# Gate products of a hybrid encoder block: nine instead of eight of sixteen row pairs by seven products, three of them with sums made by transfers

## Chip, cores, metric

The kernel runs on one core of one Trainium2 chip. The metric is the device time of one execution in microseconds (us); the kernel before has a median of 2029.64 us in three runs (2028.74 to 2030.21). The engines are named as the profile names them: PE (TensorE, matmuls), DVE (VectorE), ACT (ScalarE), POOL (GpSimd), SP (SyncE, which issues nearly all transfers).

## What is computed

One layer of a streaming encoder over 256 rows of 4096 columns:

```
xn = RMSNorm(x)
q, k, v, z_a, a_c, g_c, z_c = split(xn @ w_in)          # seven blocks of 2048 columns
y_a = RMSNorm(chunked_attention(q, k, v)) * silu(z_a)
y_c = RMSNorm(conv_module(a_c, g_c, ...)) * silu(z_c)    # ends with "@ w_pw + b_pw"
h = x + concat(y_a, y_c) @ w_out
h = h + sigmoid(RMSNorm(h) @ w_ple_gate + b) * (p @ w_ple)
out = RMSNorm(h)
```

The change concerns the two **gates** z_a and z_c: 256 x 4096 times 4096 x 2048 each.

## The kernel before

**Products.** All operands are split into a high part (rounded to fp32r) and a low part (the rest), and a product is three matmuls: high x high, low x high, high x low. The left operand is kept in SBUF, transposed, as tiles `big_t` of four blocks of 128 columns, in both parts. A weight block of 128 rows by two column blocks of 512 is loaded from HBM into `wt`, split by ACT (`wh`, L204) and DVE (`wl`, L205), and used at once. `wt` has 5 buffers, `wh` and `wl` have 3.

**Seven products.** `mixed_product` computes 256 rows by two column blocks of 512. It walks over 16 pairs of weight blocks (w0, w1). For a *plain* pair it makes 8 products (24 matmuls of 128x512, L385). For a pair marked `*` it makes seven products by a scheme of Strassen's kind (21 matmuls), P1 to P7, in the order P1, P5, P7, P2, P3, P6, P4. The three matmuls of one product take the high part, the low part of the left operand, and the low part of the weight or sum. For this DVE forms sums of weight blocks in two tiles: `ua` (w0's column blocks added, L467, and one of w0 and one of w1 added, L468) and `ub` (L474, L475). Both are split like weights (`uh` and `ul`, two buffers each). P5 and P7 read `ua`, P6 and P4 read `ub`, P1 reads w0, P2 and P3 read w1. The left side needs combinations of the blocks of x, made once per pair by `combine_again` (L291, then four operations of 128 columns at L268 to L271, then a split at L276 and L277).

**Transferred sums.** A pair marked `+` is also made by seven products, but its `ua` comes from two transfers: SP loads one summand (L420), then POOL issues an accumulating transfer that adds the other (L421). `sums_ahead` asks for them up to two pairs ahead, right behind the loads of the pair at hand. Of w0 only one column block is loaded then. Products ahead of the gates use such pairs; the gates do not.

**Order of the work.** An order is written out as a string; the gates use `dense`, `1 0* 3 2* 5 4* 6* 7 8* 9 10* 11 12* 14* 13 15`: eight pairs by seven products. A scheduler turns the program into one queue for each engine; within a queue the order is fixed. The stages around the change are: the products for attention and convolution, the product with `w_pw` (two calls of `mixed_product`, its left operand in `uS`, four big tiles of the pool `more`), then the combinations of x for pairs 4 to 14, then `gated` four times (two column pairs of z_a, two of z_c), and the product with `w_out`. The gates' sums `ua` and `ub` both come from the pool `lpool` with two buffers. At the end of a gate product DVE takes the four accumulators (L1067) and ACT applies silu (L1068). The multiplication with y (L184) is put into a list `later` and issued during the next product. At the start of the first gate product its four accumulators must first be emptied of the last `w_pw` product (L1043).

In the last gate product `y_ahead` makes the first operand of `w_out`, `yT[0]`, at the last pair of the order. It takes the fourth buffer of `more`.

Of the kernel before, what the change touches and what calls it, by code (L numbers as in the profile page):

```python
# [10 lines left out]
F32 = mybir.dt.float32  # L11
F32R = mybir.dt.float32r
# [4 lines left out]
P = 128  # L17
NB = 512
# [7 lines left out]
def hybrid_block(  # L26
# [310 lines left out]
    norm = units("1 3 5 7 9 11 0+ 13 2* 15 4+ 8 6* 10 12 14")  # L337
    norm_fills = (7, 8, 8, 8, 6, 4, 2, 3, 2, 3, 2, 2, 0, 6, 5, 5)
    final = units("1 0* 3 2* 5 4* 6* 7 8* 9 10* 12* 11 13 14 15")
    late = units("1 3 5 7 9 11 13 15 0* 2 4* 6 8* 10* 12 14")  # L340

    def mixed_product(
        w, col, lhs, comb, order, on_helpers, ahead=None, fills=(0,), on_begin=None, apart=NB,
        left=(), begin=None, after_sevens=lambda: None,
    ):


# [58 lines left out]
        def sums_ahead(n):  # L406
            for m in range(n, min(n + 3, len(order))):
                if order[m][1] != "+" or m in sums:
                    continue
                ua = sums[m] = upool.tile([P, 2, NB], F32, tag="u", name="ua")  # L410
                rows = w[2 * order[m][0] * P : (2 * order[m][0] + 1) * P, :]
                step = P * rows.ap[0][0]

                def columns(first, step):
                    return bass.AP(
                        tensor=rows.tensor, offset=rows.offset + first,
                        ap=[list(rows.ap[0]), [step, 2], [1, NB]],
                    )

                nc.sync.dma_start(ua, columns(col + apart, 0))  # L420
                nc.gpsimd.dma_start(ua, columns(col, step + apart), accum_op=ALU.add)  # L421
# [7 lines left out]
        for n, (pair, seven) in enumerate(order):  # L429
            if n < done:  # L430
                continue
            if ahead:
                ahead(pair)
            wts = []
            for k in range(2):
                wt = wpool.tile([P, 2, NB], F32, tag="w", name="wt")
                if seven == "+" and k == 0:
                    nc.sync.dma_start(wt[:, 0], w[2 * pair * P : (2 * pair + 1) * P, col : col + NB])
                else:
                    nc.sync.dma_start(wt, two_columns(w, 2 * pair + k, col, apart))  # L440
                wts.append(wt)
            sums_ahead(n)
            if n >= len(order) - n_left:
                for k in range(2):
                    tiles = left[2 * (n - len(order) + n_left) + k]
                    held.append((2 * pair + k, parts_of(wts[k], 2, tiles and tiles())[0]))
                fill(fills[n % len(fills)])
                continue
            if not seven:
                for k in range(2):  # L450
                    add_plain(n, k, *parts_of(wts[k], 2)[0])
                fill(fills[n % len(fills)])
                continue
            begins = not helper
            if begins:
                for name in ("P1", "P5", "P7", "P6"):
                    helper[name] = ps_tmp.tile([P, NB], F32, tag="tmp", name=f"acc_{name}")
                banks.update(helper)
            w0, w1 = wts
            plus = partial(nc.vector.tensor_tensor, op=ALU.add)  # L460
            before = list(recent)
            w0h, w0l = parts_of(w0, 1)[0]
            if seven == "+":
                ua = ub = sums[n]
            else:
                ua = ub = upool.tile([P, 2, NB], F32, tag="u", name="ua")
                plus(ua[:, 0], w0[:, 0], w0[:, 1])  # L467
                plus(ua[:, 1], w0[:, 1], w1[:, 1])  # L468
            with queued_behind(before if seven == "+" else ()):
                uah, ual = pair_parts(ua)  # L470
            w1h, w1l = parts_of(w1, 2)[0]
            if seven == "*" and not sums:
                ub = upool.tile([P, 2, NB], F32, tag="u", name="ub")
            plus(ub[:, 0], ua[:, 0], w1[:, 1])  # L474
            plus(ub[:, 1], ub[:, 0], w1[:, 0])  # L475
            ubh, ubl = pair_parts(ub)
            first = len(made)

            def s_of(i):
                t, at = comb[pair] if isinstance(comb, dict) else (comb[pair // 4], pair % 4)  # L480
                return [t[:, at + i // 2, q, (i % 2) * P : (i % 2 + 1) * P] for q in range(2)]

            k0, k1 = 2 * pair, 2 * pair + 1
            add("P1", block(k0, 0), (w0h[:, 0], w0l[:, 0]), n, True)
            add("P5", s_of(1), (uah[:, 0], ual[:, 0]), n, True)
            add("P7", s_of(0), (uah[:, 1], ual[:, 1]), n, True)
            add("P2", block(k1, 0), (w1h[:, 0], w1l[:, 0]), n, True)
            add("P3", s_of(3), (w1h[:, 1], w1l[:, 1]), n, True)
            add("P6", s_of(2), (ubh[:, 0], ubl[:, 0]), n, True)
            add("P4", block(k1, 1), (ubh[:, 1], ubl[:, 1]), n, True)  # L490
            if begins and on_begin:
                on_begin()
            if begins:
                tc.add_manual_dep(
                    made[first].ins, last_transpose[0].ins.name,
                    mybir.DependencyInfo(mybir.DependencyClass.NoSync, mybir.DependencyReason.DATA),
                    reason="transposes before the helpers take their banks",
                )
            if n == last_seven:
                on_helpers(helper)  # L500
                after_sevens()
            fill(fills[n % len(fills)])
# [270 lines left out]
    def layer_norm_swish():  # L773
# [67 lines left out]
        def split(c, i):  # L841
            if i == 0:
                assert more is not None
                uS.append(big_tile(more))
            hi, lo = uS[c][:, i, 0, :], uS[c][:, i, 1, :]
            nc.scalar.copy(hi, conv[c][:, i, :])
            nc.vector.tensor_tensor(lo, conv[c][:, i, :], hi.bitcast(F32), ALU.subtract)
# [107 lines left out]
    def heads(*parts, order=None, fills=early_fills, **kw):  # L955
# [6 lines left out]
        for (o, g), t in zip(parts, tiles):  # L962
            if o == o_v:
                vs[g] = t
            else:
                (queries_of if o == o_q else keys_of)(g, t)

    def open_late():

        nonlocal more  # L970
        first_sums.close()
        more = pool("more", 4)

    n_g = H // GH
    assert n_g == CW // NB == 4
# [69 lines left out]
        y_c.extend(ys)  # L1045
    nc.scalar.activation(idle_out, ssq_c[:, 0, 1:2], AF.Silu)
    r_c = rstd_of(ssq_c, CW, "r_c")


    xS = [xS[0][0]]  # L1050
    for c in range(2, D // NB):
        if c % 2 == 0:
            comb_tile(xS, 1)
        combine_again(xS[c // 2], 2 * (c % 2), xT[c], 0, sum_rows())()

    def gated(ys, c0, col, r_y, order, ahead):

        _, z = sum_tiles()

        def on_helpers(helper):  # L1060
            nc.scalar.copy(z[0][0], helper["P1"])
            helper_sums(helper, z)

        acc = mixed_product(w_in0, col + c0 * NB, xT, xS, order, on_helpers, ahead=ahead, fills=(2,))
        for h, j in QUARTERS:
            zz, y = z[h][j], ys[c0 + j][:, h]
            tt(zz, acc[h][j], zz, ALU.subtract if j else ALU.add)  # L1067
            nc.scalar.activation(zz, zz, AF.Silu, scale=r_x[:, h : h + 1])  # L1068
            if len(y.shape) == 3:
                zz = zz.rearrange("q (g d) -> q g d", d=HD)  # L1070
            later.append(partial(stt, y, y, r_y[:, h : h + 1], zz, ALU.mult, ALU.mult))

    def before_last(make):

        return lambda pair: make(0) if pair == dense[-1][0] else None

    yT, yS = [], []

    def y_ahead(pair):
        while len(yT) < min(pair // 2 + 2, D // NB):  # L1080
            c = len(yT)
            if c == D // NB - 2:
                fill(len(later))
            y, g, at = (y_a[c], ga, 4 * c) if c < len(y_a) else (y_c[c - len(y_a)], gc, 4 * (c - len(y_a)))
            operand(
                y, g[:, at : at + 4], c, yT, yS, None if c else more, combined=c < D // NB - 1
            )
        if pair == late[9][0]:

# [3 lines left out]
            )  # L1093
            later.append(lambda: rest.pop()())

    for ys, o_z, r_y in ((y_a, o_za, r_a), (y_c, o_zc, r_c)):
        for c0 in range(0, len(ys), 2):
            last = ys is y_c and c0 + 2 == len(ys)
            gated(
                ys, c0, o_z, r_y, dense,  # L1100
                before_last(y_ahead) if last else None,
            )


# [5 lines left out]
    def embedding():  # L1110

        pin = spool.tile([P, NH, PLE], F32, tag="row", name="pin", bufs=3)
        nc.sync.dma_start(pin, p[0, 0].rearrange("(h q) n -> q h n", q=P))
        pT.append(big_tile(more))
        for b, pt in enumerate(transposed(pin, range(PLE // P))):
            split_from_psum(pT[0], b, pt, 1.0)

# [234 lines left out]
```

## Time and profile before

| what | us |
|---|---|
| median of three runs | 2029.64 |
| the profiled execution's own time | 2028.23 |
| its span (first to last instruction) | 2026.5 |
| mean clock granted to TensorE | 0.998 |
| gate products, from 986 to about 1313 in the span | four of about 82 each |

All positions given later are us from the start of the span. The profiled execution lies 1.41 us below the median of the runs. Differences are worked out in the profiled execution and then applied to the median. A matmul's listed duration (390 ns) overlaps the next one's: their distance, not their duration, is what they cost. The same holds, more weakly, for DVE: one instruction's listed duration overlaps the next by some 80 ns.

### The profile page before, as it was taken

Reading aid. Unit: us, or ns where it says so; the run is one execution under the profiler, and the core shown is the slowest. Engines: PE = TensorE matmul, PEld = TensorE weight load, DVE = VectorE, ACT = ScalarE, POOL = GpSimd, SP = SyncE. Lnnn points to the kernel's source line nnn. Section 1 sums busy time; section 2 is a strip of 40 time slices with the busy share of each in tenths; the row PEclk is TensorE's granted clock in tenths of the full one; section 3 lists DMA queues with packets and bytes.
Section 4 is the critical chain, followed back from the end, with each engine's and each line's share of the span. In section 5 each row is a group of like instructions: output and inputs, shape, how many; then the busy total and the mean of one; then the engine's idle time right before and its main releaser. Section 6 shows DMA issues by size and latency. Waiting matters only on the chain.

```text
span 2026.5 us, 26195 instructions
## 1 busy us (share of the span) xinstructions
PE 2010.8 (99%) x9073; PEld 1654.4 (82%) x9073; DVE 1903.4 (94%) x2708; ACT 1215.0 (60%) x1583; POOL 46.9 (2%) x50
## 2 busy tenths in 40 slices
PE   9999999999999999999999999999999999999997
PEld 7888888888888888788888888888888888888876
DVE  7999999889999997888899999999999999999998
ACT  7655545655655555776556556666665666655555
POOL 0000000000000000000000000000000000000000
PEclk9999999999999999999999999999999999999999
DMA  8787878678678867456666666676666656666765
GB/s 295 222 238 234 255 217 250 177 247 240 188 221 246 252 198 241 156 177 209 196 208 207 208 204 211 208 239 210 203 211 197 208 194 201 208 218 207 231 207 180
DMA packets 171168, 436.70 MB, mean 215 GB/s; under 512 B 13966, under 2 KB 17182, under 8 KB 171034
## 3 DMA queue, kind: packets, MB, share of 16 engines
q1 hardware_dynamic: 161952, 417.93, 63.9%
q0 software_dynamic: 8432, 16.25, 4.8%
q8 instruction: 71, 1.16, 0.2%
q10 hardware_dynamic: 650, 0.84, 0.1%
q14 instruction: 63, 0.52, 0.1%
HBM read 430.77 MB, written 4.19 MB: 215 GB/s over the span
## 4 chain that ended last, share of the span: by engine, by line
PE 95%; DVE 3%; issue 1%; ACT 1%; DMA 0%; POOLq 0%; POOL 0%; ACTq 0%; SPq 0%; DVEq 0%
PE acc L385 73%; PE acc_P L385 17%; PE tmp_ps L170 1%; DVE cv L724 1%; PE acc L229 1%; DVE wl L205 1%; PE tmp_ps L893 0%; PE tmp_ps L877 0%; PE tmp_ps L911 0%; PE tmp_ps L916 0%; PE acc L373 0%; ACT wh L204 0%; PE tmp_ps L892 0%; DVE ul L205 0%; DMA xin<-in_x_dram 0%
## 5 line engine op out<-in xcount | busy, mean ns | idle before, releaser
L385 PE MATMUL acc<-wh,big_t 128*128 128x512 f32 x4154 | 1283.3, 391 | 0.6 <-DVE y_c L1043 0.4
L204 ACT CAST wh<-wt 128x1024 fp32r<-128x1024 f32 (+1 forms) x737 | 710.1, 974 | 523.3 <-PE acc L385 364.3
L385 PEld LDWEIGHTS acc<-wh,big_t 128*128 128x128 f32 x4154 | 777.0, 188 | 160.8 <-DVE y_c L1043 0.9
L205 DVE TENSOR_TENSOR wl<-wt,wh 128x1024 fp32r<-128x1024 f32 (+1 forms) x737 | 817.4, 1122 | 39.9 <-ACT wh L204 33.6
L385 PE MATMUL acc<-wl,big_t 128*128 128x512 f32 x2077 | 801.9, 391 | 0.1
L385 PEld LDWEIGHTS acc<-wl,big_t 128*128 128x128 f32 x2077 | 389.5, 188 | 82.5 <-DVE wl L205 1.8
L204 ACT CAST uh<-ua 128x1024 fp32r<-128x1024 f32 x174 | 182.9, 1052 | 91.1 <-DVE ua L468 46.3
L205 DVE TENSOR_TENSOR ul<-ua,uh 128x1024 fp32r<-128x1024 f32 x174 | 212.0, 1219 | 9.6 <-ACT uh L204 8.1
L724 DVE SCALAR_TENSOR_TENSOR cv<-uT,dw,cv 128x250 f32<-128x250 f32 (+19 forms) x480 | 203.6, 464 | 1.1
L385 PE MATMUL acc_P<-uh,big_t 128*128 128x512 f32 x528 | 161.8, 392 | 0.0
L204 ACT CAST uh<-ub 128x1024 fp32r<-128x1024 f32 x92 | 96.8, 1052 | 95.5 <-DVE ub L475 79.2
L205 DVE TENSOR_TENSOR ul<-ub,uh 128x1024 fp32r<-128x1024 f32 x92 | 112.2, 1220 | 6.7 <-ACT uh L204 5.6
L385 PEld LDWEIGHTS acc_P<-uh,big_t 128*128 128x128 f32 x528 | 98.0, 188 | 23.2 <-ACT uh L204 3.7
L385 PE MATMUL acc_P<-ul,big_t 128*128 128x512 f32 x264 | 101.3, 392 | 0.0
L467 DVE TENSOR_TENSOR ua<-wt 128x512 f32<-128x512 f32 x102 | 69.9, 685 | 17.3 <-DMA wt<-in_w_in_dram 10.7
L385 PE MATMUL acc<-uh,big_t 128*128 128x512 f32 x266 | 82.5, 390 | 0.0
L385 PE MATMUL acc_P<-wh,big_t 128*128 128x512 f32 x266 | 82.1, 389 | 0.0
L468 DVE TENSOR_TENSOR ua<-wt 128x512 f32<-128x512 f32 x102 | 69.6, 683 | 4.3 <-DMA wt<-in_w_in_dram 3.6
L385 PE MATMUL acc_P<-uh,comb_t 128*128 128x512 f32 x228 | 70.1, 390 | 0.1
L475 DVE TENSOR_TENSOR ub<-ub,wt 128x512 f32<-128x512 f32 x92 | 63.0, 685 | 0.8
L474 DVE TENSOR_TENSOR ub<-ua,wt 128x512 f32<-128x512 f32 x92 | 62.9, 683 | 0.3
L385 PEld LDWEIGHTS acc_P<-ul,big_t 128*128 128x128 f32 x264 | 49.3, 188 | 12.5 <-DVE ul L205 2.0
(243 smaller groups left out, 1485.5 us busy)
## 6 DMA issues: line engine op xcount, KB each, us to landing
wt<-in_w_in_dram SPq DMA_DIRECT2D x416, 512.0 KB, 4.5
wt<-in_w_out_dram SPq DMA_DIRECT2D x128, 512.0 KB, 4.3
wt<-in_w_ple_gate_dram SPq DMA_DIRECT2D x128, 512.0 KB, 4.2
wt<-in_w_pw_dram SPq DMA_DIRECT2D x32, 512.0 KB, 4.8
ua<-in_w_in_dram SPq DMA_DIRECT2D x31, 512.0 KB, 4.3
ua<-in_w_in_dram POOLq DMA_DIRECT2D x31, 512.0 KB, 8.7
wt<-in_w_in_dram SPq DMA_DIRECT2D x31, 256.0 KB, 2.8
hc<-in_x_dram SPq DMA_DIRECT2D x8, 512.0 KB, 4.7
```

The costliest lines, as they stand in the source:

```text
L170: nc.tensor.transpose(pt[:, i * T + h * P : i * T + (h + 1) * P], src[:, h, b] if len(src.shape) == 4 else src[:, h, b * P : (b + 1) * P], ...
L204: nc.scalar.copy(wh[:, :kc, :], wt[:, :kc, :]),
L205: nc.vector.tensor_tensor(wl[:, :kc, :], wt[:, :kc, :], wh[:, :kc, :].bitcast(F32), ALU.subtract),
L229: nc.tensor.matmul(acc, a, b[:, k, :], start=kb == 0 and kind == 0, stop=kb == kblocks - 1 and kind == 2,)
L385: nc.tensor.matmul(banks[name], a, b, start=name not in begun, stop=final and ends[name] == n and kind == 2 and not (left and name in "P2 ...
L467: plus(ua[:, 0], w0[:, 0], w0[:, 1])
L468: plus(ua[:, 1], w0[:, 1], w1[:, 1])
L474: plus(ub[:, 0], ua[:, 0], w1[:, 1])
L475: plus(ub[:, 1], ub[:, 0], w1[:, 0])
L724: nc.vector.scalar_tensor_tensor(cv[:, i, PAD - k :], uT[:, i, : T + k - PAD], dw[:, b, k : k + 1], cv[:, i, PAD - k :], ALU.mult, ALU.add,)
```

## The change

The gates' order becomes `nine`: nine pairs by seven products, of which 4, 10 and 15 (`4+`, `10+`, `15+`) have transferred sums. Pair 15 becomes a pair by seven products, and for it a ninth combination of x is made once, after the others. Room for it comes from `more`, which shrinks from four to three buffers. The fourth place becomes a pool of its own that is used three times in turn: first for the fourth tile of `uS` (`more_last`), then for the ninth combination and a single buffer for the transferred sums (`gate_place`), then for `yT[0]` and later the embedding's tile (`y_place`). `ub` in the gates is always a fresh tile of `lpool`.

```diff
+    nine = units("1 0* 3 2* 4+ 6* 5 8* 7 10+ 12* 9 14* 15+ 11 13")
...
-                ua = sums[m] = upool.tile([P, 2, NB], F32, tag="u", name="ua")
+                ua = sums[m] = (sums_in or upool).tile([P, 2, NB], F32, tag="u", name="ua")
...
-            if seven == "*" and not sums:
+            if (seven == "*" and not sums) or sums_in:
                 ub = upool.tile([P, 2, NB], F32, tag="u", name="ub")
...
-                uS.append(big_tile(more))
+                uS.append(big_tile(more if c < 3 else last_more[0][1]))
...
-        more = pool("more", 4)
+        more = pool("more", 3)
+        last_more.append(last_place("more_last"))
...
+    last_more.pop()[0].close()
+    gate_place, gate_pool = last_place("gate_place")
...
+    xS = {2 * c: (xS[c // 2], 2 * (c % 2)) for c in range(D // NB)}
+    xS[15] = gate_pool.tile([P, 2, 2, T], F32R, tag="ninth", name="comb_x"), 0
+    combine_again(*xS[15], xT[7], 2, sum_rows())()
...
-        acc = mixed_product(w_in0, col + c0 * NB, xT, xS, order, on_helpers, ahead=ahead, fills=(2,))
+        acc = mixed_product(
+            w_in0, col + c0 * NB, xT, xS, order, on_helpers, ahead=ahead, fills=(2,),
+            sums_in=gate_pool,
+        )
...
+    def open_y(pair):
+
+        gate_place.close()
+        last_more.append((None, pool("y_place", 1)))
+        y_ahead(pair)
...
-                ys, c0, o_z, r_y, dense,
-                before_last(y_ahead) if last else None,
+                ys, c0, o_z, r_y, nine,
+                before_last(open_y, nine) if last else None,
```

More of the change, by code (lines that the diff above doesn't have):

```diff
@@ L343, in mixed_product @@
         w, col, lhs, comb, order, on_helpers, ahead=None, fills=(0,), on_begin=None, apart=NB,
-        left=(), begin=None, after_sevens=lambda: None,
+        left=(), begin=None, after_sevens=lambda: None, sums_in=None,
     ):
@@ L966, in heads, with last_place @@
                 (queries_of if o == o_q else keys_of)(g, t)
+    last_more = []
+    def last_place(name):
+        place = ExitStack()
+        return place, pool(name, 1, place)
     def open_late():
@@ L1071, in gated, with before_last @@
             later.append(partial(stt, y, y, r_y[:, h : h + 1], zz, ALU.mult, ALU.mult))
-    def before_last(make):
-        return lambda pair: make(0) if pair == dense[-1][0] else None
+    def before_last(make, order=dense):
+        return lambda pair: make(0) if pair == order[-1][0] else None
     yT, yS = [], []
@@ L1085, in y_ahead @@
             operand(
-                y, g[:, at : at + 4], c, yT, yS, None if c else more, combined=c < D // NB - 1
+                y, g[:, at : at + 4], c, yT, yS, None if c else last_more[0][1], combined=c < D // NB - 1
             )
@@ L1113, in embedding @@
         nc.sync.dma_start(pin, p[0, 0].rearrange("(h q) n -> q h n", q=P))
-        pT.append(big_tile(more))
+        pT.append(big_tile(last_more[0][1]))
         for b, pt in enumerate(transposed(pin, range(PLE // P))):
```

## The prediction

> **What bounds the kernel now.** I read the page's head first, then the busy times of the four gate products, then who waited in them.
>
> ```profile
> PE 2010.8 (99%) x9073; PEld 1654.4 (82%) x9073; DVE 1903.4 (94%) x2708; ACT 1215.0 (60%) x1583; POOL 46.9 (2%) x50
> ...
> PE 95%; DVE 3%; issue 1%; ACT 1%; DMA 0%; POOLq 0%; POOL 0%; ACTq 0%; SPq 0%; DVEq 0%
> ```
>
> PE is busy 99% and carries 95% of the chain that ended last; DVE is busy 94%. A busy PE row alone proves little, because its durations overlap. So the next view cuts the gate stage into stretches of 81.60 us; its columns are length, PE, PEld, DVE, ACT, POOL busy, granted clock, DMA share, GB/s. The last row is an earlier stage with transferred sums, for comparison.
>
> ```profile
> 987.30:1068.90 81.60, 81.60 (x360) 67.57 (x361) 75.92 (x91) 50.02 (x58) 0.69 (x1) 1.00 0.64 204
> 1068.90:1150.50 81.60, 81.60 (x362) 67.57 (x361) 78.59 (x94) 49.37 (x55) 0.00 (x0) 1.00 0.65 208
> ...
> 629.00:680.00 51.00, 50.98 (x228) 41.98 (x228) 51.00 (x84) 25.21 (x27) 2.74 (x3) 1.00 0.83 246
> ```
>
> A gate product has 8 x 21 + 8 x 24 = 360 matmuls, and 81.60/360 = **0.2267 us** is one matmul at full clock. DVE is busy 78.59 of 81.60: 3.0 us a product are free. Who waited, first for PE (980 to 1319), then for DVE (1068 to 1319):
>
> ```profile
> PE acc L385 <- DVE y_c L1043: 0.4, 1, 0.4
> ```
> ```profile
> DVE ua L467 <- DMA wt<-in_w_in_dram: 4.7, 5, 1.5
> DVE wl L205 <- ACT wh L204: 2.8, 6, 0.7
> ```
>
> PE waits once, 0.4 us at the start of the gates, and then never: the stage is PE's. DVE is the close second.
>
> **The change part by part.**
>
> *Matmuls.* Each gate product has nine sevens: 9 x 21 + 7 x 24 = 357. Four products save 12 matmuls: 12 x 0.2267 = **-2.72 us**, all on the path. This is most of what can be gained.
>
> *DVE's work.* What an instruction occupies is the distance to the next in a full queue:
>
> ```profile
> 1084.05 1.22 DVE L205 TENSOR_TENSOR ul<-ub,uh 128x1024 fp32r<-128x1024 f32 x1
> ...
> 1085.79 2.35 DVE L205 TENSOR_TENSOR wl<-wt,wh 128x1024 fp32r<-128x1024 f32 x2
> 1088.06 0.69 DVE L468 TENSOR_TENSOR ua<-wt 128x512 f32<-128x512 f32 x1
> 1088.66 0.69 DVE L205 TENSOR_TENSOR wl<-wt,wh 128x512 fp32r<-128x512 f32 x1
> ```
>
> Two wide splits (1024) take 2.27, so **1.135** each; a sum or narrow split (512) takes **0.605**. A plain pair costs DVE two wide splits, 2.27, and PE 24 x 0.2267 = 5.44. A `*` pair costs three wide and five narrow, 6.43, and PE 4.76. A `+` pair saves two narrow, 5.22. Before: 8 x 6.43 + 8 x 2.27 = 69.6 a product; after: 6 x 6.43 + 3 x 5.22 + 7 x 2.27 = 70.1. DVE gains 0.5 while PE's product shrinks to 357 x 0.2267 = 80.9, so 3.0 us free become 1.8: on average it still fits. ACT (50 of 82) is not close.
>
> *The third seven in a row.* The average is not what counts; DVE's lead over PE is. A plain pair adds 3.17 to it, a `*` takes 1.67, a `+` 0.46. `dense` never has more than two sevens in a row; `nine` has `2* 4+ 6*`. After its sixth pair the lead gained since the start is 0.87 us; after 6* in `dense`, one plain pair later, it is 2.83. Here is how little was left at that place in the second product (DVE's split of 6*'s second sum, and PE's first matmul that reads it):
>
> ```profile
> 1100.98 1.22 DVE L205 TENSOR_TENSOR ul<-ub,uh 128x1024 fp32r<-128x1024 f32 x1
> ```
> ```profile
> 1102.80 0.39 PE L385 MATMUL acc_P<-ul,big_t 128*128 128x512 f32 x1
> ```
>
> It ended at 1102.20 and was read at 1102.80: 0.6 us to spare. For the new order I count from 2*, which both orders reach in the same way: its second sum's split started at 1084.05 (quoted), its low part was read at:
>
> ```profile
> 1087.84 0.39 PE L385 MATMUL acc_P<-ul,comb_t 128*128 128x512 f32 x1
> ```
>
> In the changed program's DVE queue, from behind that split to the end of 6*'s second split, stand eight narrow and eight wide instructions: 8 x 0.605 + 8 x 1.135 = 13.92. Among the wide ones are both splits of plain pair 5, which the scheduler put ahead of 6*'s last. So that split ends at 1084.05 + 1.135 + 13.92 + 0.09 (its tail) = 1099.20. PE reads 42 matmuls after 1087.84; but the scheduler also moved six other matmuls ahead of this one (five in the first product): 48 x 0.2267 = 10.88, at 1098.72. DVE is **0.5 us late**, once in each of products 2 to 4: +1.5. Bounds: 0 (a few tenths in either sum) and 1.8 a product (0.5 plus the 1.36 of the six matmuls, if what was moved ahead is late too).
>
> *The start of the gates, first product.* PE lost time as it entered the stage, waiting for DVE to empty an accumulator:
>
> ```profile
> 985.78 0.39 PE L385 MATMUL acc<-wl,big_t 128*128 128x512 f32 x1
> 986.00 0.61 PE L385 MATMUL acc<-wh,big_t 128*128 128x512 f32 x2
> 986.46 0.39 PE L385 MATMUL acc<-wl,big_t 128*128 128x512 f32 x1
> 987.28 0.73 PE L385 MATMUL acc<-wh,big_t 128*128 128x512 f32 x2 [0.43 <-DVE y_c L1043]
> 987.85 0.39 PE L385 MATMUL acc<-wl,big_t 128*128 128x512 f32 x1
> ```
>
> The row of 985.78 is w_pw's last matmul, 986.00 the gates' first. From 986.46 three distances took 1.39 instead of 0.68: 0.71 lost. The new queue issues the four L1043 in a row, with a wide split behind them that stood between them before:
>
> ```profile
> 981.33 0.69 DVE L468 TENSOR_TENSOR ua<-wt 128x512 f32<-128x512 f32 x1 [0.98 <-DMA wt<-in_w_in_dram]
> ...
> 984.81 0.68 DVE L1043 TENSOR_TENSOR y_c<-acc,row 128x512 f32<-128x512 f32 x1
> 985.41 1.21 DVE L205 TENSOR_TENSOR wl<-wt,wh 128x1024 fp32r<-128x1024 f32 x1
> 986.55 1.88 DVE L1043 TENSOR_TENSOR y_c<-acc,row 128x512 f32<-128x512 f32 x3
> ...
> 989.59 0.16 DVE L551 TENSOR_REDUCE r_c<-ssq_c 128x2 f32<-128x8 f32 x1
> 989.78 0.17 DVE L138 TENSOR_SCALAR r_c<-r_c 128x2 f32<-128x2 f32 x1
> ```
> ```profile
> 967.65 0.28 DVE L268 TENSOR_TENSOR comb<-comb 128x128 f32<-128x128 f32 x1
> 967.85 0.28 DVE L269 SCALAR_TENSOR_TENSOR comb<-comb 128x128 f32<-128x128 f32 x1
> ```
>
> The ninth combination puts about 1.4 us ahead of them (one narrow, four of 128 columns at 0.2, the distance in the last two rows), of which the idle 0.98 at 981 takes most; they start at about 985.3, and each accumulator is free before PE comes. I take **-0.71** (bounds -0.71 and 0). From 985.3 the new queue needs 14 narrow, eight wide and r_c's two (0.4), 17.95, to the end of 2*'s second split, and seven narrow and eight wide, 13.32, from there to the end of 6*'s: 1016.6. PE, without its wait, reads there at 986.0 + 2 x 5.44 + 3 x 4.76 + 22 x 0.2267 = 1016.15: 0.45 late. On top comes the first transferred sum:
>
> ```profile
> ua<-in_w_in_dram SPq DMA_DIRECT2D x31, 512.0 KB, 4.3
> ua<-in_w_in_dram POOLq DMA_DIRECT2D x31, 512.0 KB, 8.7
> ```
> ```profile
> 983.78 0.33 SPq L440 DMA_DIRECT2D wt<-in_w_in_dram  x1
> ...
> 986.65 0.33 SPq L440 DMA_DIRECT2D wt<-in_w_in_dram  x1
> ```
>
> Its place is that of `uS`'s fourth tile, so SP, behind the load of 983.78, waits for the last w_pw matmul, 985.78 + 0.39 = 986.2. With 4.3 and 8.7, and some tenths for two issues, it has landed at about 999.5 to 1000.5; DVE wants it at 985.3 + 14.5 (12 narrow, six wide and r_c's 0.4) = 999.8. I add 0.5: **+1.0** in the first product (bounds 0 and 2.2). The next weight load, which SP issued at 986.65, moves by some 0.2, and five `wt` buffers cover that; POOL's r_c waits behind the accumulate, and nobody reads r_c before the third product.
>
> *Transfers.* Direct ones cost 63.9% of the span for 417.93 MB, accumulating ones 4.8% for 16.25 MB:
>
> ```profile
> q1 hardware_dynamic: 161952, 417.93, 63.9%
> q0 software_dynamic: 8432, 16.25, 4.8%
> ```
>
> That is 3.1 and 6.0 us of all engines per MB. A `+` adds 0.26 MB net of direct and 0.52 MB of accumulating transfer, 3.9 us; three a product lift the share from 0.65 to 0.80. In the row from 629 to 680 above it was 0.83 with PE at 50.98 of 51.00. The later sums are asked for some 14 us and more before DVE's use, one buffer being free as soon as the sum before is split; I cost them at nothing. [...]
>
> *The rest.* The three-buffer pool gives the later tiles places that are long free; `yT[0]` waits for 15+, which PE passes a plain pair earlier. Both 0.
>
> **Sum.** -2.72 - 0.71 + 1.0 + 1.5 = **-0.9**: 2028.23 becomes 2027.3, and the median 2029.64 becomes **2028.7**.
>
> **Rivals.**
>
> *B, DVE is never late.* PE has no new wait: -3.43, 2026.2. For it: no PE wait in the gates now, and 0.5 is the difference of two sums of 11 and 14 us. Against it: only 0.6 was to spare with two sevens in a row.
>
> *C, DVE becomes the bound at 6*; slower.* Loads land later in busier queues (4.0 us in the gates, 4.6 from 300 to 930, where sums were transferred):
>
> ```profile
> wt<-in_w_in_dram SPq DMA_DIRECT2D x121, 512.0 KB, 4.0
> ```
> ```profile
> wt<-in_w_in_dram SPq DMA_DIRECT2D x186, 512.0 KB, 4.6
> ```
>
> DVE's sums L467 stand early in its queue and block it while they wait for a load; from 987 to 1300, in us and times:
>
> ```profile
>   DMA wt<-in_w_in_dram: 8.0, 10
> ```
>
> Ten waits each 0.6 longer are 1.5 a product. If all falls ahead of 6*, it is -3.43 + 2.5 + 3 x 2.0 = +5.1, 2034.7. It decides from 0.86 us of PE wait a product. Against it: in my count the loads of 4+, 6* and 5 land some 4 us ahead of use.
>
> *D, the first sum lands late.* The slowest accumulate took 9.9 instead of 8.7: 1.2 more in the first product, 2029.9.
>
> ```profile
> DMA to landing us min/median/max: 6.5/8.7/9.9
> ```
>
> That the change doesn't happen is no rival: the built queues hold the 12 matmuls less.
>
> **How the numbers follow.** Forecast 0.50, B 0.20, C 0.20, D 0.07, something not foreseen 0.03. A measurement of this kernel tells about 0.2%, 4.06 us, from no change: 2025.6 to 2033.7 is "same". Forecast, B, D and a fifth of C (a wait between 0.86 and 1.8 a product) lie inside: 0.81. Slower: 0.17, C's other four fifths and 0.01 of the unforeseen. Faster: the other 0.02, since all that can go here is 3.43 us. The range, 2025.9 to 2033.0, runs from B less 0.3 of the runs' own spread to the lower part of C, leaving out about 2 in 10.
>
> **What would show it.** Gate products of 357 matmuls in 80.9 us plus a wait; PE waits put down to DVE `ul` or `ub` at 6*, four times, about 0.5 each and 1.0 in the first; no wait for L1043; DMA share near 0.80. I am wrong if PE waits at another pair, if it waits for nothing, or if DVE's idle in the gates grows.

## The result, and the profile after

The changed kernel takes **2036.77 us** (median of seven runs, 2033.85 to 2038.18); the kernel before, on the same chip, 2029.91 us (2028.74 to 2032.04). The ratio is 1.0032 with a 95% interval of 1.0022 to 1.0042: slower by 6.9 us, where 1 us less was forecast, and above the range. The profiled execution is the fastest of the seven (2033.85 us, span 2032.1), so the trace shows the mild form: 5.6 us more of span than before. What the other runs lost beyond that, 2.9 us in the median, no trace here shows.

The page's busy line and its chain:

```profile
PE 2011.4 (99%) x9061; PEld 1652.8 (81%) x9061; DVE 1908.6 (94%) x2714; ACT 1223.1 (60%) x1592; POOL 62.3 (3%) x62
...
PE 92%; DVE 4%; issue 2%; DMA 1%; ACT 1%; POOLq 0%; POOL 0%; ACTq 0%; DVEq 0%
```

The 12 matmuls are gone (9061 for 9073). PE's share of the chain fell from 95% to 92%, and DMA has a share at all. The page doesn't say where; what PE waited for between 930 and 1340 does (total us, times, longest):

```profile
PE acc L386 <- DVE z L1084: 3.7, 3, 2.7
PE acc_P L386 <- DVE ul L205: 1.4, 3, 0.7
PE acc_P L386 <- ACT uh L204: 0.7, 1, 0.7
```

L1084 is the drain: four DVE instructions at a product's end that take the sums out of the accumulators (L1067 before). PE waits for it three times, at the start of products 2, 3 and 4; before, never. The rows of PE there and at the third seven in a row:

```profile
1007.75 0.50 PE L386 MATMUL acc_P<-ul,big_t 128*128 128x512 f32 x1 [0.70 <-DVE ul L205]
...
1015.83 0.74 PE L386 MATMUL acc_P<-uh,big_t 128*128 128x512 f32 x2 [0.72 <-ACT uh L204]
...
1068.26 0.39 PE L386 MATMUL acc<-wl,big_t 128*128 128x512 f32 x1
1069.11 0.70 PE L386 MATMUL acc<-wh,big_t 128*128 128x512 f32 x2 [0.47 <-DVE z L1084]
1069.65 0.40 PE L386 MATMUL acc<-wl,big_t 128*128 128x512 f32 x1
...
1096.25 0.50 PE L386 MATMUL acc_P<-ul,big_t 128*128 128x512 f32 x1 [0.33 <-DVE ul L205]
...
1150.71 0.39 PE L386 MATMUL acc<-wl,big_t 128*128 128x512 f32 x1
1151.67 0.70 PE L386 MATMUL acc<-wh,big_t 128*128 128x512 f32 x2 [0.57 <-DVE z L1084]
1152.21 0.39 PE L386 MATMUL acc<-wl,big_t 128*128 128x512 f32 x1
...
1178.81 0.50 PE L386 MATMUL acc_P<-ul,big_t 128*128 128x512 f32 x1 [0.33 <-DVE ul L205]
...
1233.27 0.39 PE L386 MATMUL acc<-wl,big_t 128*128 128x512 f32 x1
1236.37 0.84 PE L386 MATMUL acc<-wh,big_t 128*128 128x512 f32 x2 [2.71 <-DVE z L1084]
1237.00 0.63 PE L386 MATMUL acc<-wl,big_t 128*128 128x512 f32 x1
1237.43 1.05 PE L386 MATMUL acc<-wh,big_t 128*128 128x512 f32 x2
1238.28 0.63 PE L386 MATMUL acc<-wl,big_t 128*128 128x512 f32 x1
...
1239.99 0.72 PE L386 MATMUL acc<-wh,big_t 128*128 128x512 f32 x2
1240.55 0.40 PE L386 MATMUL acc<-wl,big_t 128*128 128x512 f32 x1
```

What a wait costs is read from distances of starts, not from the bracket at a row's end. From 1068.26 to 1069.65 run three matmuls, 0.68 us at 0.2267; it took 1.39, so 0.71 is lost, though the bracket says 0.47. In product 3 it is 0.82. In product 4, twelve matmuls (2.72) took 7.28: **4.56 lost**. Of these, 2.9 are the pause itself (3.10 from start to start), and 1.7 come because for some 4 us after the pause a matmul took 0.43 us instead of 0.2267. Together the three starts cost 6.1 us. That is about as much as the whole delay, since the other losses and gains nearly cancel (point 8 below).

Why the drain is late is to be read on DVE, ahead of it:

```profile
1226.48 0.69 DVE L468 TENSOR_TENSOR ua<-wt 128x512 f32<-128x512 f32 x1 [1.19 <-DMA wt<-in_w_in_dram]
...
1231.33 0.69 DVE L469 TENSOR_TENSOR ua<-wt 128x512 f32<-128x512 f32 x1 [2.42 <-DMA wt<-in_w_in_dram]
1231.94 0.68 DVE L475 TENSOR_TENSOR ub<-ua,wt 128x512 f32<-128x512 f32 x1
1232.66 0.69 DVE L476 TENSOR_TENSOR ub<-ub,wt 128x512 f32<-128x512 f32 x1
1233.27 1.22 DVE L205 TENSOR_TENSOR wl<-wt,wh 128x1024 fp32r<-128x1024 f32 x1
1234.40 1.22 DVE L205 TENSOR_TENSOR ul<-ua,uh 128x1024 fp32r<-128x1024 f32 x1
1235.54 2.48 DVE L1084 TENSOR_TENSOR z<-acc,z 128x512 f32<-128x512 f32 x4
```

L468 and L469 are the sums of the **next** product's first pair, 0*. The scheduler put them ahead of this product's drain. They stand 1.19 and 2.42 us for the two loads of 0*, with the drain queued behind. In the kernel before the same order stood there, and the loads came nearly in time (L467 and L468 are the same two sums, L1067 the drain):

```profile
1223.52 0.69 DVE L467 TENSOR_TENSOR ua<-wt 128x512 f32<-128x512 f32 x1 [0.19 <-DMA wt<-in_w_in_dram]
...
1225.90 0.69 DVE L468 TENSOR_TENSOR ua<-wt 128x512 f32<-128x512 f32 x1
...
1230.11 2.47 DVE L1067 TENSOR_TENSOR z<-acc,z 128x512 f32<-128x512 f32 x4
```

The queues of SP and POOL show what came between (the row of 1218.82 holds three loads; the last two, at 1222.08 and 1223.99, are those of 0*):

```profile
1217.50 0.38 SPq L421 DMA_DIRECT2D ua<-in_w_in_dram  x1
1218.82 5.50 SPq L441 DMA_DIRECT2D wt<-in_w_in_dram  x3
```
```profile
1223.45 1.22 POOL L422 DMA_DIRECT2D ua<-in_w_in_dram  x1 [22.22 <-DVE z L514]
```

The request at 1217.50 is for the sum of 4+, four pairs later; the accumulating half of it leaves POOL at 1223.45, between the two loads that DVE needs first. The five weight loads that SP issued between 1216 and 1230 landed after (min/median/max us), in the changed kernel and then in the one before:

```profile
DMA to landing us min/median/max: 4.4/5.3/7.3
```
```profile
DMA to landing us min/median/max: 3.4/3.8/4.3
```

The 7.3 is the second load of 0*: issued at 1223.99, landed at 1231.3, which is when L469 starts.

### The profile page after: what moved, and what is told of

Its sections match the earlier page's. It is cut to its first block, busy times and chain, and to the rows that moved or that the text cites. A ratio compares the mean times of both kernels' runs of the same rounds, so it can differ in the third digit from the quotient of the medians.

```text
span 2032.1 us, 26246 instructions
## 1 busy us (share of the span) xinstructions
PE 2011.4 (99%) x9061; PEld 1652.8 (81%) x9061; DVE 1908.6 (94%) x2714; ACT 1223.1 (60%) x1592; POOL 62.3 (3%) x62
## 4 chain that ended last, share of the span: by engine, by line
PE 92%; DVE 4%; issue 2%; DMA 1%; ACT 1%; POOLq 0%; POOL 0%; ACTq 0%; DVEq 0%
PE acc L386 70%; PE acc_P L386 17%; DVE wl L205 1%; DVE cv L725 1%; PE tmp_ps L170 1%; DMA wt<-in_w_in_dram 1%; PE acc L229 1%; DVE ul L205 1%; PE tmp_ps L894 0%; PE tmp_ps L878 0%; PE tmp_ps L912 0%; PE tmp_ps L917 0%; PE acc L374 0%; ACT wh L204 0%; PE tmp_ps L893 0%
## 5 line engine op out<-in xcount | busy, mean ns | idle before, releaser
L386 PE MATMUL acc<-wh,big_t 128*128 128x512 f32 x4098 | 1267.9, 392 | 3.9 <-DVE z L1084 3.7
L386 PEld LDWEIGHTS acc<-wh,big_t 128*128 128x128 f32 x4098 | 767.1, 188 | 162.8 <-ACT wh L204 4.1
L386 PE MATMUL acc<-wl,big_t 128*128 128x512 f32 x2049 | 791.6, 392 | 0.1
L386 PEld LDWEIGHTS acc<-wl,big_t 128*128 128x128 f32 x2049 | 384.6, 188 | 81.2 <-DVE wl L205 1.4
L204 ACT CAST uh<-ua 128x1024 fp32r<-128x1024 f32 x178 | 187.1, 1052 | 109.6 <-DVE ua L469 63.2
L205 DVE TENSOR_TENSOR ul<-ua,uh 128x1024 fp32r<-128x1024 f32 x178 | 216.9, 1219 | 10.1 <-ACT uh L204 9.3
L204 ACT CAST uh<-ub 128x1024 fp32r<-128x1024 f32 x96 | 101.0, 1052 | 78.3 <-DVE ub L476 66.2
L205 DVE TENSOR_TENSOR ul<-ub,uh 128x1024 fp32r<-128x1024 f32 x96 | 117.1, 1220 | 7.5 <-ACT uh L204 6.8
L422 POOL DMA_DIRECT2D ua<-in_w_in_dram x43 | 52.6, 1222 | 975.6 <-DMA ua<-in_w_in_dram 284.8
L468 DVE TENSOR_TENSOR ua<-wt 128x512 f32<-128x512 f32 x94 | 64.4, 685 | 13.0 <-DMA wt<-in_w_in_dram 8.4
L469 DVE TENSOR_TENSOR ua<-wt 128x512 f32<-128x512 f32 x94 | 64.3, 684 | 5.2 <-DMA wt<-in_w_in_dram 5.1
```

The lines of the kernel that those rows point to most:

```text
L204: nc.scalar.copy(wh[:, :kc, :], wt[:, :kc, :]),
L205: nc.vector.tensor_tensor(wl[:, :kc, :], wt[:, :kc, :], wh[:, :kc, :].bitcast(F32), ALU.subtract),
L386: nc.tensor.matmul(banks[name], a, b, start=name not in begun, stop=final and ends[name] == n and kind == 2 and not (left and name in "P2 ...
```

## The experiments

**Theory 1**: the traffic of a transferred sum, asked for too early, delays the next product's first loads; DVE's queue stands still for them ahead of the drains. **Theory 2**: nine pairs by seven products simply are more than DVE can do beside 80.9 us of PE, at 6* above all. Differences below are of medians, against runs of the kernel before on the same chip.

**Order of the pairs.** Eight pairs by seven products as before, three of them with transferred sums:

```diff
-    nine = units("1 0* 3 2* 4+ 6* 5 8* 7 10+ 12* 9 14* 15+ 11 13")
+    nine = units("1 0* 3 2* 4+ 6* 5 7 8* 9 10+ 11 12* 14+ 13 15")
```

> The gates go back to eight pairs by seven products, but three of them keep transferred sums in the same place and at the same points of the order (4+ fifth, 10+ tenth; 14+ in the place of 15+). VectorE has about 3.6 us less work in each product than in the kernel before (six narrow sums of 0.605 us). Theory 1 (the traffic of the transferred sums makes the loads of the next product's pair 0 late, and VectorE's queue waits for them ahead of the four instructions that empty the accumulators): TensorE still waits at the starts of products 2 to 4, 1 to 4 us in all, and the time is 1 to 6 us above before. Theory 2 (VectorE simply has too much work in the gates, at 6* above all): no wait, time within 0.5 us of before.

2042.9 us, ratio 1.0067 (1.0052 to 1.0082): worse than either theory allows. With 14+ only three pairs behind 10+ and one buffer for the sums, other things broke as well (SP stood 44.6 us for DVE's splits ahead of narrow loads, 8.1 in the changed kernel), so this is no clean test. It does show that sums by transfer can cost 13 us where DVE has *less* to do than in the kernel before, which speaks against theory 2. DVE stood 41 us for weight loads there, but whether traffic or SP's late issue made them late isn't shown.

```diff
+    nine = units("1 0* 3 2* 5 4+ 6* 7 8* 10+ 9 12* 14* 15+ 11 13")
```

> The changed kernel with an order that has no three sevens in a row near the start: 1 0* 3 2* 5 4+ 6* 7 8* 10+ 9 12* 14* 15+ 11 13. Theory 2: the waits at 6* (2.1 us in the changed kernel's profile) go away and most of the loss with them, 2030 to 2034. Theory 1: only those 2.1 us go, the waits at the product starts stay as they are, 2034 to 2036.

2033.16, ratio 1.0017 (1.0008 to 1.0027). That is 3.1 of the 6.9 us back, and inside the range of theory 2, not of theory 1. The trace says more than the time: the waits at 6* are gone, those for the drain stay (1.29, 1.50 and 0.76 us, 3.6 in all for 3.7 before the edit), and `ul`, the low part of a sum, brings new ones in products 1 and 2 (1.55 and 0.55). No half-speed matmuls follow here. So the third seven in a row is a real cost, but a kernel without it still waits for its drains and is still 3.8 us behind.

**The drain first.** The first sums of a product (L468, L469) are queued behind the last drain of the product before:

```diff
+            emptied = list(drains) if begins else []
...
+                with queued_behind(emptied):
                     plus(ua[:, 0], w0[:, 0], w0[:, 1])
                     plus(ua[:, 1], w0[:, 1], w1[:, 1])
...
+            drains[:] = [tt(zz, acc[h][j], zz, ALU.subtract if j else ALU.add)]
```

> The changed kernel, with the next product's sums for pair 0 queued on VectorE behind the last instruction that empties the accumulators, instead of ahead of it. Theory 1: the waits at the product starts (0.5, 0.6 and 2.7 us in the changed kernel's profile) and the half-speed matmuls behind the longest go away, 4 to 6 us less than the changed kernel: 2030.5 to 2032.5; the waits at 6* (0.3 to 0.7 each) stay. Theory 2: the order of these few instructions does not matter, 2036 to 2037.

2030.67, ratio 1.0007 (0.9998 to 1.0017): 5.6 us of the 6.9 are back, as theory 1 expected, and no wait for a drain is left.

**The request later.** `pin` keeps SP's request for a sum behind the weight loads that the program names before it; nothing else changes:

```diff
-                nc.sync.dma_start(ua, columns(col + apart, 0))
+                first = nc.sync.dma_start(ua, columns(col + apart, 0))
+                if sums_in:
+                    pin(first)
```

> The changed kernel with each transferred sum's first transfer kept behind the weight loads that stand ahead of it in the program: the request for the next product's 4+ moves from behind that product's first load to behind its sixth. Theory 1: pair 0's loads land in time, the waits at the product starts go away, 2030.5 to 2033. Theory 2: unchanged, 2036 to 2037. A third outcome, worse than 2037: the sum itself then lands too late for 4+.

2029.2, ratio 1.0001 (0.9992 to 1.001): 7.1 us back by a later place for the sums' requests on SP. Its queue near the same boundary, the landing of the four weight loads that SP issued there between 1216 and 1230, and PE's waits from 980 to 1340:

```profile
1223.45 7.45 SPq L443 DMA_DIRECT2D wt<-in_w_in_dram  x3
1230.95 0.43 SPq L421 DMA_DIRECT2D ua<-in_w_in_dram  x1
```
```profile
DMA to landing us min/median/max: 3.5/3.6/3.9
```
```profile
PE acc_P L386 <- ACT uh L204: 0.8, 1, 0.8
PE acc_P L386 <- DVE ul L205: 0.4, 1, 0.4
PE acc L386 <- DVE z L1086: 0.4, 1, 0.4
```

The request moved from 1217.50 to 1230.95. The bytes of the stage are the same and the DMA share of a product is 0.78 (0.77 before the edit): what changed is not how much is transferred, but when.

**What in the request costs?** First GpSimd's accumulating transfer is left out in the gates (so twelve sums lack an addend), with SP's request still early. Then it is there again, but as a plain copy over the first addend (twelve sums are one addend alone):

```diff
-                nc.gpsimd.dma_start(ua, columns(col, step + apart), accum_op=ALU.add)
+                if not sums_in:
+                    nc.gpsimd.dma_start(ua, columns(col, step + apart), accum_op=ALU.add)
```

> The changed kernel with GpSimd's accumulating transfer left out in the gates: SP still asks for the first addend of each sum at the same place of its queue, the second addend is not added, so twelve sums lack it. If it is the accumulate's traffic that makes the next product's first loads late (theory 1a), the boundary waits go and the time is 2028 to 2031. If it is the place of the request in SP's queue, its own load and SP standing still for its buffer (theory 1b), the waits stay at about 1 to 2 us each and the time is 2032 to 2036. Theory 2 (DVE's work alone): no change from the changed kernel, 2034 to 2037.

```diff
-                nc.gpsimd.dma_start(ua, columns(col, step + apart), accum_op=ALU.add)
+                if sums_in:
+                    nc.gpsimd.dma_start(ua, columns(col, step + apart))
+                else:
+                    nc.gpsimd.dma_start(ua, columns(col, step + apart), accum_op=ALU.add)
```

> The changed kernel with GpSimd's second transfer kept in place, queue and size in the gates, but as a plain copy over the first addend instead of an accumulation, so twelve sums are one addend alone. If it is the bytes that delay the next product's first loads, the boundary waits stay: 2032 to 2036. If it is the accumulating kind, which takes 6.0 instead of 3.1 us of the 16 engines per MB, they shrink to about half or go: 2028.5 to 2031.5.

Without it 2029.38, ratio 1.0003 (0.9994 to 1.0012); as a plain copy 2034.24, ratio 1.0025 (1.0016 to 1.0035). PE's waits for the drain in the first and in the second:

```profile
PE acc L386 <- DVE z L1085: 0.2, 1, 0.2
```
```profile
PE acc L386 <- DVE z L1087: 3.3, 2, 1.7
```

So it is the second 512 KB on top of the first that makes the loads late, not SP's place alone; a plain copy costs 5.1 us, an accumulation 6.9 (the slowest weight load issued between 1216 and 1230 takes 5.2, 6.0 and 7.3 us without it, with a copy, with an accumulation). The bet on the accumulating kind was wrong. That SP also stands still for the single buffer (10.8 us in seven waits) costs nothing by itself: it does so in the run without the second transfer too (11.4 us).

**No transfers at all.** All nine pairs `*`:

> Nine sevens a product with all sums on DVE: no transferred sum in the gates, three more sums and splits of 0.605 us each a `+` pair less, DVE some 3.6 us a product more than in the changed kernel, 82 against PE's 80.9. Theory 1: no late load at the boundary, PE waits for DVE's splits and drains by what DVE lacks, 1 to 2 us a product: 2030 to 2036. Theory 2 (DVE's work is what cost the time): clearly slower than the changed kernel, 2038 and more.

2032.51, ratio 1.0017 (1.0008 to 1.0026). This is against theory 2: with some 3.6 us *more* work for DVE in each product, by the expectation's count, the kernel is faster than the changed one, which loses 6.9. DVE is busy 80.1 to 81.2 of 82 us in the products, PE's listed waits are 1.3 us in all, and the kernel is 3.6 us slower than before: hardly any of DVE's time is free here. Transferred sums that come at the right time (2029.2 above, 0.2 us under its base) are worth 3.8 us against that.

**Both mends and their limits.** First the late request and the order of 2033.16 together:

> Both edits together: the sums' request stays behind the weight loads ahead of it, and 4+ and 6* are parted by a plain pair. Theory 1 (the early request makes the next product's first loads late; 6* is a second, separate and smaller cost): the boundary waits go, as with the late request alone, and so do the 0.4 to 0.8 us waits at 6*; the 1.6 and 0.6 us waits that this order brought in products 1 and 2 may stay. 2026.5 to 2029, PE waits in the gates under 2.5 us in all. Theory 2 (DVE simply has too much work in the gates, wherever it stands): the waits come back elsewhere, 2029 to 2031, no better than the late request alone at 2029.2.

2042.08, ratio 1.0063 (1.005 to 1.0077), far outside both expectations. Now the request was too late: DVE stood 3.4 to 4.6 us in products 2 to 4 for the sum of 4+ itself (14.6 us in four waits), because DVE was ready for 4+ of the last product 12 us after SP issued its request (19 us in the run of 2029.2), while the sum's two transfers took 16. Asked for one pair earlier:

```diff
-            for m in range(n, min(n + 3, len(order))):
+            for m in range(n, min(n + (4 if sums_in and not sums else 3), len(order))):
```

> The order without three sevens in a row and the late request, as in the run of 2042.1 us, but 4+ of each product asked for one pair earlier in SP's line. There DVE stood 3.4 to 4.6 us for the sum of 4+ itself, in products 2 to 4. If a transferred sum has a window (asked for too early its traffic delays the next product's first loads, too late it is itself late), those waits go and with them some 8 us: 2030 to 2035, what is left being waits for loads. If the sum was late for another reason (busy queues), it is still late: 2038 to 2043.

2030.89, ratio 1.0011 (1.0002 to 1.002): those waits are gone, 11 us with one place in a queue. Here 4+ of the last product came 19 us after its request, in the changed kernel 37. So the transferred sums had a window with two sides: 12 us ahead of DVE's use was too late, 19 was in time, and 37 made the loads beside them late. Then the late request and the drain first, in the changed kernel's own order:

> The changed kernel's own order, late request, and the next product's first sums behind the drains. Theory 1: the last 0.4 us of boundary wait go, the 0.8 and 0.4 us at 6* stay, so 2028 to 2029.5, level with before or a little under. Theory 2: the boundary wait comes back as a wait for DVE's splits behind the drains, 2029 to 2031.

2030.21, ratio 1.0003 (0.9994 to 1.0012): in the range of theory 2, not of theory 1. With the order `1 0* 3 2* 5 4+ 6* 7 8* 10+ 9 12* 11 14* 15+ 13`, both mends took 2032.16 (1.0017, 1.0008 to 1.0026), above what either expected, with PE waits of 1.3 us for `ul` in product 1 and 0.95 for the last drain:

> Late request, the next product's first sums behind the four drains of this one, and an order without three sevens in a row or two * pairs beside each other ahead of a +. Theory 1: no PE wait over 0.5 us in the gates; what is left is the saving of 12 matmuls and the 0.4 to 0.7 us at the start: 2026 to 2028. Theory 2: DVE's lead runs out somewhere else, 2029 to 2031.

In the run of 2030.21 PE is listed with one wait of 0.5 us from 980 to 1320, yet the time is that of before. What its weight loads (PEld) waited for in the same stretch says why (in the kernel before they waited once there, for the old drain):

```profile
PEld acc_P L386 <- ACT uh L204: 6.3, 22, 0.9
PEld acc L386 <- DVE z L1088: 0.7, 3, 0.2
PEld acc L386 <- DVE wl L205: 0.6, 3, 0.2
```

22 times a weight load had to wait for `uh`, the high part of a sum, whose chain is DVE's sum and ACT's split. Such a wait cost PE about 0.1 us that no bracket of PE shows: between 986 and 1316, some 40 distances of starts are 0.02 to 0.15 us too long, 3.3 us together, and all but three of them lie beside a listed wait of a weight load; in the kernel before two are too long, 0.2 us. That is more than the 2.7 us of the matmuls.

**DVE relieved.** To see whether DVE's work eats the saving, the 16 multiplications that apply the gates to y are left out (y stays ungated), in the run with both mends, in the kernel before and in the changed kernel:

```diff
-            later.append(partial(stt, y, y, r_y[:, h : h + 1], zz, ALU.mult, ALU.mult))
```

> Late request and drains first (the run of 2030.2 us), without the final multiplications of the gates (the 16 instructions that scale y and multiply it by the gate; y stays ungated): DVE has four instructions of 0.6 to 0.7 us a product less. If DVE's short lead is what eats the saving of matmuls (theory 2 in its small form), the short waits of weight loads for split halves go and the time falls to 2026 to 2028, some 2.5 to 3.4 us under the former kernel relieved in the same way. If something else eats it, the two relieved kernels are level.

> The kernel before without the same 16 multiplications: PE waits nowhere in its gates, so relief of DVE should bring nothing there: 2028 to 2029.5 by both theories, at most 0.4 us less for the wait at the start and some tenths behind the gates, where the last of these multiplications stand. It is the base for the other two.

> The changed kernel without the same 16 multiplications. Theory 1: the late loads ahead of the drains are not mended by a lighter DVE, the boundary waits stay, at 1 us or more each, and the time is 2031 to 2035. Theory 2 (too much work for DVE): the waits go with the relief, 2026 to 2029, level with the run that has both mends.

2028.69 (0.9996, 0.9987 to 1.0005), 2028.94 (0.9999, 0.999 to 1.0008) and **2035.25** (1.0027, 1.0016 to 1.0039). The third decides against theory 2: with DVE relieved the changed kernel is still 6.3 us behind its base, the relieved kernel before, and PE still waits for the drain, as its view from 980 to 1345 says:

```profile
PE acc L386 <- DVE z L1084: 3.9, 3, 2.9
```

The first two leave the small question half open. By the relief the kernel with both mends went from 1.1 us above the kernel before to 0.5 below. Its short waits for `uh` fell from 22 to four, but nine for `ul` stand in their place, and it is level with its base, not 2.5 us below, which by its expectation points to another cause. DVE's short lead seems to take part of the saving; that it takes all of it isn't shown. No version tried beats the kernel before by more than the measurement's 0.2%.

**The half-speed matmuls.** Extra DVE instructions ahead of the drain in the kernel before, 2, 3 and 4 of them at the ends of products 1 to 3:

```diff
+        held_up = [tt(junk, acc[0][0][:, : NB // 2], z[0][0][:, : NB // 2], ALU.max) for _ in range(extra.pop(0))]
...
+            with queued_behind(held_up):
```

> The kernel before, with two, three and four extra DVE instructions of 256 columns (into a tile that nobody reads) queued ahead of the four drains at the ends of gate products 1, 2 and 3; DVE's other work interleaves, so PE should pause about 1.4, 2.8 and 3.8 us. If a pause of PE above some 2 us is what brought the half-speed matmuls of the changed kernel, the second and third pause are followed by matmuls at about 0.43 us for some 3 us, the first is not: span 2026.5 + 8.0 + about 3.6, 2038. If the slow matmuls had another cause, all three pauses are followed by 0.227 us at once: about 2034.5.

A miss: PE had three matmuls of another accumulator in front, no listed pause was over 0.53 us, and the one run took 2032.17. With the matmuls of each product's first two pairs held in their order:

> As the earlier run with extra DVE instructions ahead of the drains in the kernel before, but the matmuls of each gate product's first two pairs keep their traced order, so PE has nothing to put in front of the accumulators it waits for: pauses of about 1.6, 3.0 and 4.0 us at the ends of products 1 to 3. If the pause itself brings half speed, the second and third are followed by matmuls about 0.43 us apart for some 3 us each, the first by 0.227 us. If not, all three by 0.227 us.

One run, 2040.84 (span 2039.1). The pauses were 1.05, 2.69 and 3.92 us; the second and the third:

```profile
1152.12 0.39 PE L385 MATMUL acc<-wl,big_t 128*128 128x512 f32 x1
1155.20 0.70 PE L385 MATMUL acc<-wh,big_t 128*128 128x512 f32 x2 [2.69 <-DVE z L1074]
1155.74 0.40 PE L385 MATMUL acc<-wl,big_t 128*128 128x512 f32 x1
1155.97 0.62 PE L385 MATMUL acc<-wh,big_t 128*128 128x512 f32 x2
...
1240.99 1.19 PE L385 MATMUL acc<-wh,big_t 128*128 128x512 f32 x2 [3.92 <-DVE z L1074]
1241.98 0.63 PE L385 MATMUL acc<-wl,big_t 128*128 128x512 f32 x1
1242.40 1.05 PE L385 MATMUL acc<-wh,big_t 128*128 128x512 f32 x2
1243.26 0.63 PE L385 MATMUL acc<-wl,big_t 128*128 128x512 f32 x1
```

After 3.92 us the matmuls run 0.43 us apart; after 2.69 us they run at 0.227 at once, which the expectation did not allow, though the changed kernel's 2.71 us was followed by half speed. So a pause can bring it, and near 2.7 us it does not depend on the length alone.

## Why the prediction was wrong, point by point

1. *Matmuls, -2.72.* Right in count: 9073 to 9061. The price fits the sum in point 8; no run measures it alone.
2. *The start of the gates, -0.71.* Right: no wait for the old drain at 986 is left.
3. *First product, +1.0.* By distances of starts 2.0 were lost. The wait at 6* is there (0.72 for 0.45). The other (0.70 at 1007.75) comes from a wait of DVE: it stood 1.31 us, until 1000.53, for a weight load of 4+ beside the first accumulating transfer. The step and rival D had the sum itself landing late. It did, by some 0.4 us (issued at 990.0, landed 9.6 later, DVE was free at 999.2), but the weight load came last. Without that transfer neither wait is listed.
4. *The third seven in a row, +0.5 in products 2 to 4.* The mechanism was right and the size near: 0.33 in products 2 and 3, nothing listed in 4; by distances of starts, which take in the late matmul behind each wait, 0.6, 0.6 and 0.2. These waits stay when the accumulating transfer is left out and go when the three are parted: a count of DVE's queue was good to 0.2 us.
5. *Transfers: "I cost them at nothing".* **This step failed**, by 6.1 us at three product starts, 1.7 of it half-speed matmuls. It took the share of busy DMA (0.65 to 0.80 forecast, 0.77 measured) and one early stretch where 0.83 did PE no harm as proof. It looked at whether the sums would land in time, not at what their bytes do to the loads beside them, and it didn't look up where in SP's queue the requests stood: the order of the built queues showed them, between the loads of the next product's first pairs. The weight loads at the last boundary took 3.4 to 4.3 us before and up to 7.3 after. The prediction's own sign came true: PE waits at another place than 6*, the drains.
6. *Rival C (2034.7, 0.20)* had the mechanism, loads that land later and DVE's sums standing in front of other work, and nearly the price, the price by luck: it put the wait at 6*, where the loads had some 4 us to spare by the prediction's count; it was at the product's end, where DVE's queue held the next product's sums ahead of the drain. The quoted DVE waits for loads, 8.0 us in ten, were the sign: no slack against a later load, wherever one of them stood ahead of something that PE needs.
7. *Rival D (2029.9, 0.07)* counted on a first sum that lands after 9.9 instead of 8.7 us. It took 9.6; the transferred sums of the gates landed after 8.4 us (median), those of the kernel before after 8.7, with DVE 94% busy in both. PE's wait at 1007.75 came from a weight load, not from the sum (point 3).
8. The sum: -2.72 - 0.71 + 2.0 + 1.4 + 6.1 = +6.1, against a last drain that starts 6.2 us later in the trace (1324.48 for 1318.31).

## What to carry to other kernels

A transfer issued ahead had two prices in these runs: it could come too late (14.6 us of waits in one order), and it made its neighbours in the queue late (a weight load took 7.3 us, before 4.3 at most). Look up between which loads it is issued and what waits for those, and give it a place behind the loads whose consumers stand first in an in-order queue; here a later place on SP was worth 7 us, and in another order one pair too late cost 11. With PE and DVE within some 2 us of each other in a product (80.9 us of matmuls by the prediction's price; in the run with both mends DVE was busy 78.4 to 79.8 us in products 2 to 4), much of the work taken from PE came back here as waits that its own rows hardly show: add up the distances of starts, and read what the weight loads waited for.

## What the runs showed of the hardware

**Half speed after a pause.** At 1238 to 1242 of the changed kernel the profile's granted clock is 0.73 (a row of stretches of PE: length, busy, clock, DMA share, GB/s):

```profile
1238.00:1242.00 4.00, 4.00 (x15) 0.73 0.42 127
```

The rows above give 0.43 us a matmul for 4.0 us after 2.71 us of pause and for 5.5 us after 3.92, where the granted clock from 1241 to 1246 is 0.50; 2.69 (granted clock 1.00 from 1155 to 1159) and, in the relieved changed kernel, 2.85 us brought nothing. What decided between the nearly equal pauses of 2.69, 2.71 and 2.85 us isn't shown.

**A wait cost more than its bracket.** A listed wait of 0.33 us cost PE 0.6: the bracket leaves out some 0.15 us at its start, and the matmul after the first comes 0.1 us late. In the kernel with both mends such losses, without any bracket, made up 3.3 us.
